# A fp32 decoder layer on one core: more weight sums by DMA at both ends of the feed-forward, token differences made in its first product, tokens prepared two products ahead

## The chip, the core and the metric

One core of a Trainium2 chip runs the whole kernel. The metric is the device time of one execution in microseconds (us), the median over several runs; beside it stands a trace of one profiled execution. The engines are PE (matrix products), DVE (elementwise, also from PSUM banks), ACT (activations and copies), POOL and SP. Here SP issues the loads of weights, and POOL issues the DMAs that add one tile to another.

## What is computed

One layer on 512 tokens of width 1024 in float32: a mixing layer of three head groups, cross-attention into 256 memory tokens, and a feed-forward of width 4096, each as `x = x + RMSNorm(f(RMSNorm(x)))`. The change is in the feed-forward:

```python
h = rms_norm(x, pre_ffn_g[l])
f = jnp.square(jax.nn.relu(h @ w_ff1[l])) @ w_ff2[l]
x = x + rms_norm(f, post_ffn_g[l])
```

## The kernel before

**Arithmetic.** Each float32 operand is split into a high and a low part (`split`, L112: ACT copies the high part, DVE at L115 subtracts it for the low part), and a product is three matmuls: high by low, high by high, low by high. A weight's parts are `fhi` and `flo` of 128x1024; three pairs can live at a time (`HALVES`).

**Seven products for eight.** Both products of the feed-forward work on 2x2 blocks with seven block products p = 1 to 7. They need sums of weight quarters. With quarters r00, r01, r10, r11 the sums are t1 = r00+r01 (used at p = 5), r01 += r11 (p = 7), r00 += r01 (p = 6) and r10 += r00 (p = 4). `Block.sums` makes t1 on DVE (L895), the second sum on DVE (L897) or by a DMA add, and r00 by a DMA add. `Block.of(p)` splits the weights of p and, at p = 6, adds r10 by DMA. All DMA adds (`dma_add`, L868) are issued by POOL, in order; each is 512 KB. The quarters live in 11 slots (`RAWS`): a load waits until the slot's last user is done.

**First product** (`products1`). Eight column groups n of 512 columns, 24 matmuls of 128x256 a product. The order of the work (n, p): p = 1, 2 of groups 0 to 2 (`EARLY`), then group by group (n,5), (n-1,4), (n,6), (n,3), (n,7), from group 3 on with p = 1 and 2 in their places. Weights are prepared two products ahead (`AHEAD`). While it starts, the tokens come from the projection of the cross-attention, one 128-row tile tt at a time: `add_norm`, `norm_a` (DVE L178, then POOL L183 takes a power of one column, then DVE L204 scales two halves), and `put_ff`, which transposes and splits them (DVE L945 and L115). Each finished group is squared into `fq`, which lies in SBUF.

**Second product** (`products2`). Four chunks m of 1024 rows of w_ff2, 24 matmuls of 128x512 a product, p in the order 1, 2, 5, 3, 6, 7, 4 (2, 1, 5, 3, 6, 7, 4 in the last chunk). Its tokens are sums and differences of quarters of `fq` (DVE L1097), split one product ahead, with the weights. Six of the eight PSUM banks keep p = 2, 3, 4 over all chunks; p = 1, 5, 6, 7 share the other two and are drained after each product into `p_sum`: by ACT in chunk 0; for p = 1 and 5 of chunks 1 and 2 by an ACT copy (L1157) and a DMA add; else by a DVE add (L1159). In the last chunk DVE combines the sums into output rows (L1172, L1177), `scaled` multiplies by the gain (L570), and `add_norm` (L178, POOL L183, L577) ends a row tile.

**Order.** A scheduler lays out each engine's program once. It goes by the order of the code and by priorities (`ahead(n)` puts work forward by n), and an engine runs its program in that order: an instruction that waits holds all behind it.

Of the kernel before, what the change touches and what calls it, by code (L numbers as in the profile page):

```python
# [16 lines left out]
P = 128  # L17
# [18 lines left out]
def trunk(ctx: ExitStack, tc: tile.TileContext, a: dict, out: bass.AP):  # L36
# [132 lines left out]
    def gain(src, queue=nc.sync):  # L169
        g = gains.tile([P, D], F32, tag="gain", name=nm("gain"))  # L170
        queue.dma_start(out=g, in_=bass.AP(tensor=src.tensor, offset=src.offset, ap=[[0, P], [1, D]]))
        return g


# [695 lines left out]
    class Block:  # L870


        def __init__(self, shape, src):
            self.shape = shape
            self.src = src
            self.raw = {}

        def load(self, ats, not_before=None):
            for at in ats:
                r = self.raw[at] = self.quarter()  # L880
                with ahead(400):
                    for dst, part in self.src(*at)(r):
                        d = nc.sync.dma_start(out=dst, in_=part)
                        if not_before is not None:
                            tc.add_manual_dep(d.ins, not_before.ins.name, mybir.DependencyInfo(
                                mybir.DependencyClass.NoSync, mybir.DependencyReason.DATA), reason="room")
# [33 lines left out]
    def put_ff(xs, tt):  # L920
# [45 lines left out]
    def group(n):  # L966
# [6 lines left out]
            return parts  # L973
        return Block([P, 4, 256], src)

    def products1(xs):
        work = [(n, p) for n in range(EARLY) for p in (1, 2)]
        for n in range(GROUPS):
            one = [(n, p) for p in ((5, 6, 3, 7) if n < EARLY else (1, 5, 2, 6, 3, 7))]
            work += one[:1] + ([(n - 1, 4)] if n else []) + one[1:]  # L980
        work.append((GROUPS - 1, 4))
        blocks = {}
        ready = {}
# [3 lines left out]
        FIRST, REST = ((0, 0), (1, 0)), ((0, 1), (1, 1))
        for n in range(EARLY):
            blocks[n] = group(n)
            blocks[n].load(FIRST, ff_after[0])  # L990
        blocks[0].load(REST, ff_after[0])

        def prepare(at):

            if at >= len(work):
                return
            n, p = work[at]
            ready[at] = blocks[n].of(p)
            if p == 1 and n >= EARLY:
                blocks[n].sums(False)  # L1000
            if (n, p) == (EARLY - 1, 2):
                blocks[0].sums(False)
            if p == 6 and n + 1 < EARLY:
                blocks[n + 1].sums(False)
            if p == 5 and n + 1 < GROUPS:
                if n + 1 >= EARLY:
                    blocks[n + 1] = group(n + 1)
                    blocks[n + 1].load(FIRST)
                blocks[n + 1].load(REST)

        def out(n, p, ps):

# [31 lines left out]
                else:  # L1044
                    square(quarter(1, 0), two(ps))

        for at in range(AHEAD):
            prepare(at)
        for at, (n, p) in enumerate(work):
            if at in (1, 4):  # L1050
                put_ff(xs[at // 4 + 2], at // 4 + 2)
            prepare(at + AHEAD)
# [16 lines left out]
            out(n, p, ps)  # L1069

    def chunk(m):
        def src(q, i, j):
# [2 lines left out]
                yield t, a["w_ff2"][f:f + 2].rearrange("f p c -> p f c")[:, :, j * 512:(j + 1) * 512]  # L1077
            return parts
        return [Block([P, 2, 512], lambda i, j, q=q: src(q, i, j)) for q in range(2)]

    def products2():
        kept = {p: (bank(), bank()) for p in (2, 3, 4)}
# [26 lines left out]
        def load(m):  # L1109
            if m < NM:  # L1110
                blocks[m] = chunk(m)
                for at in ((0, 0), (1, 0), (0, 1), (1, 1)):
                    for q in range(2):
                        blocks[m][q].load([at])

        def prepare(at):
            if at < len(work):
                m, p = work[at]
                th, tl = tokens(m, p)
                ready[at] = (th, tl, [blocks[m][q].of(p) for q in range(2)])  # L1120
                if p == 1:
                    for q in range(2):
                        blocks[m][q].sums(True)
                if p == 5:
                    load(m + 1)

        load(0)
        def finish(tt, half, y):
            rows[tt][half] = scaled(y, g5[:, HALF[half]])
            if None not in rows[tt]:  # L1130
                add_norm(tt, rows[tt])
                for c in HALF:
# [134 lines left out]
```

## Time and profile before

| | us |
|---|---|
| median of 3 runs | 734.82 (734.81 to 735.44) |
| the profiled execution: its own time | 734.33 |
| its span in the trace | 732.5 |
| PE busy / DVE busy / ACT busy in the span | 695.5 / 530.2 / 433.0 |
| first matmul of the first product | 386.21 |
| first matmul of the last chunk, (3,2) | 675.05 |
| PE's last matmul ends | 717.6 |

The timeline lists instructions by their start. In brackets stands how long the engine was idle before an instruction, and who released it. PEclk is the granted TensorE clock, 1.00 for 2.4 GHz and 0.50 for 1.2 GHz. "Landing" of a DMA is counted from its issue.

### The profile page before, as it was taken

How to read it: one execution, taken by the hardware profiler on the slowest of the kernel's cores; microseconds unless marked ns; L12 is line 12 of the kernel's file. 1: busy time of each engine (PE TensorE's matmuls, PEld its weight loads, DVE VectorE, ACT ScalarE, POOL GpSimd, SP SyncE). 2: the span in 40 equal slices, each digit the busy share in tenths (PEclk: the TensorE clock that was granted, in tenths of full speed). 3: DMA queues.
4: the chain of work that ended last, by engine and by line, in shares of the span. 5: the costliest groups of instructions: out<-in, count | busy, mean ns of one | idle time of the engine just before them, and what ended most of it. 6: DMA issues, size and time to landing. Idle time of an engine off the chain costs nothing.

```text
span 732.5 us, 10699 instructions
## 1 busy us (share of the span) xinstructions
PE 695.5 (95%) x4032; PEld 609.5 (83%) x4032; DVE 530.2 (72%) x803; ACT 433.0 (59%) x776; POOL 132.3 (18%) x143
## 2 busy tenths in 40 slices
PE   8999999997999999999998799999999999999891
PEld 6777888797887889888888799999999888787681
DVE  3479999876774892464469967655666979889797
ACT  5463478797794662353457667666677667375522
POOL 4445343243200110000012010000002021110101
PEclk9999999999999999999999899999999999999997
DMA  8460412143331430011073395567569789695603
GB/s 286 177 230 29 145 40 76 59 158 131 116 114 59 144 115 30 30 57 58 1 223 94 96 221 143 151 168 172 143 179 194 214 186 251 160 247 152 116 0 115
DMA packets 45124, 96.67 MB, mean 132 GB/s; under 512 B 4113, under 2 KB 21265, under 8 KB 45074
## 3 DMA queue, kind: packets, MB, share of 16 engines
q1 hardware_dynamic: 37344, 72.36, 28.9%
q0 software_dynamic: 6336, 23.07, 17.5%
q10 hardware_dynamic: 1394, 0.57, 0.4%
q8 instruction: 31, 0.51, 0.3%
q14 instruction: 19, 0.16, 0.1%
HBM read 70.83 MB, written 2.10 MB: 100 GB/s over the span
## 4 chain that ended last, share of the span: by engine, by line
PE 68%; DVE 17%; ACT 6%; issue 4%; POOL 3%; DMA 2%; DVEq 0%; POOLq 0%; ACTq 0%
PE ps L1067 20%; PE ps L123 15%; PE ps L125 15%; PE ps L124 15%; DVE small L115 2%; DVE flo L115 2%; DVE lo L144 2%; POOL fixed L183 2%; DVE fixed L577 1%; DMA tmp<-in_w_sT 1%; PE ps L685 1%; DVE small L1097 1%; PE ps L697 1%; DVE ps L383 1%; DVE tmp L204 1%
## 5 line engine op out<-in xcount | busy, mean ns | idle before, releaser
L1067 PE MATMUL ps<-small,fhi 128*128 128x256 f32 x896 | 163.8, 285 | 2.7 <-DVE small L115 2.0
L115 DVE TENSOR_TENSOR flo<-quarter,fhi 128x1024 fp32r<-128x1024 f32 x112 | 135.5, 1220 | 38.1 <-ACT fhi L113 34.8
L1067 PEld LDWEIGHTS ps<-small,fhi 128*128 128x128 f32 x896 | 141.2, 194 | 3.8 <-DVE small L115 2.5
L1067 PE MATMUL ps<-small,flo 128*128 128x256 f32 x448 | 127.9, 286 | 3.4 <-DVE flo L115 3.4
L113 ACT ACTIVATE fhi<-quarter 128x1024 fp32r<-128x1024 f32 x112 | 115.3, 1050 | 24.8 <-PE ps L1067 17.2
L123 PE MATMUL ps<-flo,small 128*128 128x512 f32 x224 | 88.2, 394 | 3.3 <-DVE flo L115 2.4
L1067 PEld LDWEIGHTS ps<-small,flo 128*128 128x128 f32 x448 | 86.7, 194 | 4.3 <-DVE flo L115 4.2
L123 PE MATMUL ps<-xl,hi 128*128 128x512 f32 (+1 forms) x256 | 87.3, 341 | 0.5 <-DVE xl L115 0.5
L124 PE MATMUL ps<-fhi,small 128*128 128x512 f32 x224 | 87.7, 392 | 0.0
L125 PE MATMUL ps<-fhi,small 128*128 128x512 f32 x224 | 87.7, 392 | 0.0
L125 PE MATMUL ps<-xh,lo 128*128 128x512 f32 (+1 forms) x256 | 86.3, 337 | 0.4 <-DVE lo L144 0.4
L124 PE MATMUL ps<-xh,hi 128*128 128x512 f32 (+1 forms) x256 | 86.3, 337 | 0.0
L143 ACT ACTIVATE hi<-raw 128x512 fp32r<-128x512 f32 x120 | 70.1, 625 | 14.3 <-PE ps L125 6.8
L868 POOL DMA_DIRECT2D quarter<-quarter x40 | 35.3, 888 | 237.7 <-DVE flo L115 106.5
L144 POOL TENSOR_TENSOR lo<-raw,hi 128x512 fp32r<-128x512 f32 x48 | 63.2, 1331 | 75.7 <-ACT hi L143 66.4
L183 POOL TENSOR_TENSOR fixed<-fixed 128x1 f32<-128x1 f32 x30 | 19.7, 658 | 256.3 <-DVE fixed L178 237.1
L144 DVE TENSOR_TENSOR lo<-raw,hi 128x512 fp32r<-128x512 f32 x72 | 50.6, 732 | 9.7 <-ACT hi L143 9.3
L123 PEld LDWEIGHTS ps<-xl,hi 128*128 128x128 f32 x256 | 48.6, 190 | 5.7 <-issue 0.7
L125 PEld LDWEIGHTS ps<-xh,lo 128*128 128x128 f32 x256 | 48.5, 190 | 5.8 <-DVE lo L144 0.8
L123 PEld LDWEIGHTS ps<-flo,small 128*128 128x128 f32 x224 | 42.3, 189 | 13.2 <-ACT small L113 2.8
L124 PEld LDWEIGHTS ps<-xh,hi 128*128 128x128 f32 x256 | 48.6, 190 | 4.7
L123 PE MATMUL ps<-lo,feat 128*128 128x512 f32 x128 | 50.5, 395 | 0.0
(179 smaller groups left out, 1326.9 us busy)
## 6 DMA issues: line engine op xcount, KB each, us to landing
quarter<-quarter POOLq DMA_DIRECT2D x40, 512.0 KB, 5.2
quarter<-in_w_ff SPq DMA_DIRECT2D x64, 256.0 KB, 4.3
quarter<-in_w_ff SPq DMA_DIRECT2D x32, 512.0 KB, 5.0
raw<-in_w_xk SPq DMA_DIRECT2D x8, 512.0 KB, 3.2
raw<-in_w_xv SPq DMA_DIRECT2D x8, 512.0 KB, 4.2
raw<-in_w_out SPq DMA_DIRECT2D x8, 512.0 KB, 3.5
raw<-in_w_xq SPq DMA_DIRECT2D x8, 512.0 KB, 3.9
raw<-in_w_xo SPq DMA_DIRECT2D x8, 512.0 KB, 4.4
```

Source lines behind the costliest of these rows:

```text
L113: nc.scalar.activation(hi, src, AF.Copy, scale=1.0 if scale is None else scale)
L115: nc.vector.tensor_tensor(out=lo, in0=src, in1=hi.bitcast(F32), op=ALU.subtract)
L123: latest[0] = nc.tensor.matmul(ps, lhsT=lh, rhs=rl, start=start, stop=False)
L124: nc.tensor.matmul(ps, lhsT=lh, rhs=rh, start=False, stop=False)
L125: nc.tensor.matmul(ps, lhsT=ll, rhs=rh, start=False, stop=stop)
L143: nc.scalar.activation(hi, raw[:, c], AF.Copy)
L144: eng.tensor_tensor(out=lo, in0=raw[:, c], in1=hi.bitcast(F32), op=ALU.subtract)
L183: nc.gpsimd.tensor_tensor(out=r, in0=v, in1=neghalf[:, 0:1], op=ALU.pow)
L204: nc.vector.scalar_tensor_tensor(out=xn, in0=src[:, c], scalar=r, in1=g[:, c], op0=ALU.mult, op1=ALU.mult)
L383: nc.vector.scalar_tensor_tensor(out=ac[:, d:], in0=y[:, 0:S - d], scalar=wdw[:, i, CONV - 1 - d:CONV - d], in1=ac[:, d:], op0=ALU.mult, o ...
L868: nc.gpsimd.dma_start(out=out, in_=in_, accum_op=ALU.add)
L1067: nc.tensor.matmul(o, lhsT=w[:, k, c], rhs=x[:, k, :], start=first_, stop=last_, skip_group_check=True)
```

## The change

1. `load_t1`: for groups 0 to 2 of the first product and chunks 2 and 3 of the second, r00 is loaded a second time, and t1 is made from it by a DMA add of r01 instead of by DVE. For groups 0 to 2 the sum r01 += r11 is a DMA add too (`sums(True)`), and group 0's sums are asked for at (0,2), not (2,2).
2. `begin1`: the first weights are loaded and prepared from within `put_ff` of the first token tile.
3. After p = 4 of groups 1 and 3, DVE makes the differences x00-x10 (into `n3`) and x10-x11 (in place) that chunks 0 and 1 of the second product need.
4. Tokens of the second product are split two products ahead (`AHEAD_X`); weights still one.
5. The last gain is loaded in the second product, not ahead of the first.
6. In the last chunk p = 1 and 5 are drained by ACT copies and a DMA add as well.

```diff
+        def load_t1(self, after=None):
+            b00 = self.raw[0, 0]
+            self.load([(0, 0)], after)
+            self.t1, self.raw[0, 0] = self.raw[0, 0], b00
         def sums(self, by_dma):
-            self.t1 = self.quarter()
-            nc.vector.tensor_tensor(out=self.t1, in0=r[0, 0], in1=r[0, 1], op=ALU.add)
+            if self.t1 is None:
+                self.t1 = self.quarter()
+                nc.vector.tensor_tensor(out=self.t1, in0=r[0, 0], in1=r[0, 1], op=ALU.add)
+            else:
+                with ahead(400):
+                    dma_add(self.t1, r[0, 1])
...
         if tt == 0:
             ff_after[0] = latest[0]
+            begin1()
...
+        blocks1[0].load_t1(ff_after[0])
...
-            if (n, p) == (EARLY - 1, 2):
-                blocks[0].sums(False)
+        if (n, p) == (0, 2):
+            blocks1[0].sums(True)
             if p == 6 and n + 1 < EARLY:
-                blocks[n + 1].sums(False)
+            blocks1[n + 1].sums(True)
...
+            blocks1[n + 1].load(REST)
+            if n + 1 < EARLY:
+                blocks1[n + 1].load_t1()
...
+            if p == 4 and n % 2 == 1 and n // 2 < N3S:
...
+                nc.vector.tensor_tensor(out=n3s[m], in0=x00, in1=x10, op=ALU.subtract)
+                nc.vector.tensor_tensor(out=x10, in0=x10, in1=x11, op=ALU.subtract)
...
+            if m in n3s:
+                sums[m, 1], sums[m, 3] = x(1, 0), n3s[m]
...
+                if m >= 2:
+                    for q in range(2):
+                        blocks[m][q].load_t1()
...
+        for at in range(AHEAD_X):
+            prepare_x(at)
         prepare(0)
         for at, (m, p) in enumerate(work):
+            if at == NM:
+                g5.append(gain(a["post_ffn_g"], after=latest[0]))
+            prepare_x(at + AHEAD_X)
             prepare(at + 1)
...
-            part = small([P, 2, 512], F32) if 0 < m < NM - 1 and p in (1, 5) else None
+            part = small([P, 2, 512], F32) if m and p in (1, 5) else None
```

In the changed kernel line numbers are higher: L115 and L945 of the text are L115 and L959 there, L1020 is L1044, L1159 is L1205, L1172 and L1177 are L1218 and L1223, L570 and L577 are L576 and L583, L178 and L183 are L184 and L189, and the DMA adds of L868 stand at L873.

The first place is DVE's program at the start of the first product, from the L178 that belongs to the norm of token tile 2. Before:

```order
L178 TENSOR_SCALAR fixed<-fixed 128x1
L895 TENSOR_TENSOR quarter_4127<-quarter_3957,quarter_3975 128x1024
L204 SCALAR_TENSOR_TENSOR tmp_3894<-fixed,gain_row_3060 128x512
L204 SCALAR_TENSOR_TENSOR tmp_3896<-fixed,gain_row_3060 128x512
L115 TENSOR_TENSOR flo_3982<-quarter_3957,fhi_3981 128x1024
L178 TENSOR_SCALAR fixed<-fixed 128x1
L570 TENSOR_TENSOR tmp_3941<-ps_3898,gain_3058 128x512
L577 SCALAR_TENSOR_TENSOR fixed<-tmp_3705,fixed 128x512
L577 SCALAR_TENSOR_TENSOR fixed<-tmp_3941,fixed 128x512
L115 TENSOR_TENSOR flo_3986<-quarter_3960,fhi_3985 128x1024
```

With the change:

```order
L184 TENSOR_SCALAR fixed<-fixed 128x1
L210 SCALAR_TENSOR_TENSOR tmp_3930<-fixed,gain_row_3060 128x512
L210 SCALAR_TENSOR_TENSOR tmp_3932<-fixed,gain_row_3060 128x512
L184 TENSOR_SCALAR fixed<-fixed 128x1
L576 TENSOR_TENSOR tmp_3977<-ps_3934,gain_3058 128x512
L583 SCALAR_TENSOR_TENSOR fixed<-tmp_3703,fixed 128x512
L583 SCALAR_TENSOR_TENSOR fixed<-tmp_3977,fixed 128x512
L115 TENSOR_TENSOR flo_3866<-quarter_3838,fhi_3865 128x1024
L184 TENSOR_SCALAR fixed<-fixed 128x1
L115 TENSOR_TENSOR flo_3870<-quarter_3841,fhi_3869 128x1024
```

The weight sum of L895 is gone from between the norm's two steps, and the low part of a weight that stood ahead of the projection's gain product now stands behind the two sums into x.

The second place is POOL's program from the 16 powers of the norms on; the quarters' names differ, and the adds are t1, r01, r00 and r10 of a group. Before (three groups' r00 and r10):

```order
L183 TENSOR_TENSOR fixed<-fixed 128x1 x16
L868 DMA quarter_3957<-quarter_3975 128x1024
L868 DMA quarter_3960<-quarter_3957 128x1024
L868 DMA quarter_3963<-quarter_4189 128x1024
L868 DMA quarter_3966<-quarter_3963 128x1024
L868 DMA quarter_3969<-quarter_4324 128x1024
L868 DMA quarter_3972<-quarter_3969 128x1024
```

With the change:

```order
L189 TENSOR_TENSOR fixed<-fixed 128x1 x15
L873 DMA quarter_3862<-quarter_3856 128x1024
L189 TENSOR_TENSOR fixed<-fixed 128x1
L873 DMA quarter_3856<-quarter_3859 128x1024
L873 DMA quarter_3838<-quarter_3856 128x1024
L873 DMA quarter_3841<-quarter_3838 128x1024
L873 DMA quarter_4195<-quarter_4189 128x1024
L873 DMA quarter_4189<-quarter_4192 128x1024
L873 DMA quarter_3844<-quarter_4189 128x1024
L873 DMA quarter_3847<-quarter_3844 128x1024
```

Each of the first three groups now has four DMA adds in a row where it had two, and the first add stands ahead of the last power.

The third place is DVE's program in the last chunk around the last weights (the flo of p = 4, second half). Before, with the drain of p = 7 as the last two rows:

```order
L1159 TENSOR_TENSOR small_5895<-ps_7032,small_5895 128x512
L115 TENSOR_TENSOR flo_7029<-quarter_6607,fhi_7028 128x1024
L1159 TENSOR_TENSOR small_5895<-ps_7033,small_5895 128x512
L115 TENSOR_TENSOR flo_7089<-quarter_6601,fhi_7088 128x1024
L1172 TENSOR_TENSOR small_5895<-small_5893,small_5895 128x1024
L115 TENSOR_TENSOR flo_7093<-quarter_6603,fhi_7092 128x1024
L1159 TENSOR_TENSOR small_5896<-ps_7096,small_5896 128x512
L1159 TENSOR_TENSOR small_5896<-ps_7097,small_5896 128x512
```

With the change, where the drain of p = 7 is L1205:

```order
L1223 TENSOR_TENSOR small_5903<-small_5903,ps_5899 128x512
L1223 TENSOR_TENSOR small_5903<-small_5903,ps_5900 128x512
L576 TENSOR_TENSOR tmp_7081<-small_5903,gain_6121 128x512
L184 TENSOR_SCALAR fixed<-fixed 128x1
L576 TENSOR_TENSOR tmp_7092<-small_5903,gain_6121 128x512
L184 TENSOR_SCALAR fixed<-fixed 128x1
L583 SCALAR_TENSOR_TENSOR fixed<-tmp_6947,fixed 128x512
L583 SCALAR_TENSOR_TENSOR fixed<-tmp_7081,fixed 128x512
L583 SCALAR_TENSOR_TENSOR fixed<-tmp_6952,fixed 128x512
L583 SCALAR_TENSOR_TENSOR fixed<-tmp_7092,fixed 128x512
L1205 TENSOR_TENSOR small_5906<-ps_7109,small_5906 128x512
L115 TENSOR_TENSOR flo_7105<-quarter_6617,fhi_7104 128x1024
```

The last flo now stands behind the drain of p = 7 and behind the end of rows (0,·), L1223 to L583; before, it stood ahead of both.

## Rows read from the trace of the kernel before

**Rows 1.** The page, part 1: busy time, share of the span, instructions.

```profile
PE 695.5 (95%) x4032; PEld 609.5 (83%) x4032; DVE 530.2 (72%) x803; ACT 433.0 (59%) x776; POOL 132.3 (18%) x143
```

**Rows 2.** Busy time by stretch: length, busy (count) per engine, PEclk, DMA share, GB/s.

```profile
405.00:420.00 15.00, 10.51 (x67) 9.89 (x66) 14.97 (x20) 9.82 (x16) 0.87 (x1) 0.77 0.30 80
411.23:418.06 6.83, 4.40 (x21) 4.38 (x21) 6.83 (x8) 2.21 (x3) 0.00 (x0) 0.50 0.23 71
425.00:450.00 25.00, 25.00 (x210) 25.00 (x209) 16.03 (x15) 17.40 (x25) 2.12 (x3) 1.00 0.83 212
560.00:675.00 115.00, 114.15 (x504) 93.93 (x503) 99.63 (x90) 71.12 (x82) 18.49 (x21) 1.00 0.85 206
694.50:697.95 3.45, 3.45 (x10) 2.63 (x9) 3.45 (x4) 1.51 (x2) 0.00 (x0) 0.51 0.00 0
717.00:732.50 15.50, 0.59 (x3) 0.17 (x1) 11.46 (x21) 2.85 (x10) 2.52 (x4) 0.66 0.36 135
```

**Rows 3.** PE's timeline at the start: start, us, line, operation [idle before it, releaser].

```profile
410.15 1.10 PE L1067 MATMUL ps<-small,fhi 128*128 128x256 f32 x4 [1.96 <-DVE small L115]
413.68 0.58 PE L1067 MATMUL ps<-small,flo 128*128 128x256 f32 x1 [2.43 <-DVE flo L115]
```

**Rows 4.** DVE's timeline, same stretch.

```profile
384.62 1.22 DVE L895 TENSOR_TENSOR quarter<-quarter,quarter 128x1024 f32<-128x1024 f32 x1
...
395.26 1.22 DVE L897 TENSOR_TENSOR quarter<-quarter,quarter 128x1024 f32<-128x1024 f32 x1
...
409.41 2.49 DVE L115 TENSOR_TENSOR small<-xf,small 128x512 fp32r<-128x512 f32 x4
```

**Rows 5.** POOL's timeline, same stretch.

```profile
384.85 1.39 POOL L183 TENSOR_TENSOR fixed<-fixed 128x1 f32<-128x1 f32 x1 [2.92 <-DVE fixed L178]
389.09 0.55 POOL L183 TENSOR_TENSOR fixed<-fixed 128x1 f32<-128x1 f32 x1 [2.85 <-DVE fixed L178]
...
397.08 1.06 POOL L868 DMA_DIRECT2D quarter<-quarter  x1 [3.19 <-DVE xf L945]
402.43 0.87 POOL L868 DMA_DIRECT2D quarter<-quarter  x1 [4.29 <-PE ps L1067]
418.70 0.87 POOL L868 DMA_DIRECT2D quarter<-quarter  x1 [15.40 <-DVE quarter L897]
424.45 1.80 POOL L868 DMA_DIRECT2D quarter<-quarter  x2 [4.88 <-DMA quarter<-quarter]
```

**Rows 6.** Line 868, every DMA add of the run: issue to landing.

```profile
DMA to landing us min/median/max: 4.5/5.2/9.8
```

**Rows 7.** The page, part 5, high parts of weights; part 6, their loads (us to landing).

```profile
L113 ACT ACTIVATE fhi<-quarter 128x1024 fp32r<-128x1024 f32 x112 | 115.3, 1050 | 24.8 <-PE ps L1067 17.2
...
quarter<-in_w_ff SPq DMA_DIRECT2D x64, 256.0 KB, 4.3
```

**Rows 8.** DVE's timeline at the fourth column group.

```profile
436.04 1.23 DVE L895 TENSOR_TENSOR quarter<-quarter,quarter 128x1024 f32<-128x1024 f32 x1 [3.43 <-DMA quarter<-in_w_ff]
```

**Rows 9.** PE's waits in the second product: total us, times, longest.

```profile
PE ps L123 <- DVE flo L115: 2.4, 1, 2.4
PE ps L123 <- DVE small L1159: 0.9, 2, 0.4
```

**Rows 10.** PE's timeline in the last chunk: its first matmul, and the late one.

```profile
675.05 0.39 PE L123 MATMUL ps<-flo,small 128*128 128x512 f32 x1
...
693.96 0.47 PE L123 MATMUL ps<-flo,small 128*128 128x512 f32 x1 [2.44 <-DVE flo L115]
```

**Rows 11.** DVE's timeline in the last chunk.

```profile
687.93 1.29 DVE L570 TENSOR_TENSOR tmp<-small,gain 128x512 f32<-128x512 f32 x2
...
710.00 1.22 DVE L115 TENSOR_TENSOR flo<-quarter,fhi 128x1024 fp32r<-128x1024 f32 x1
...
726.58 2.74 DVE L577 SCALAR_TENSOR_TENSOR fixed<-tmp,fixed 128x512 f32<-128x512 f32 x4 [0.50 <-POOL fixed L183]
```

**Rows 12.** DMA issues from 600 to 660 us: adds of partial sums, landing.

```profile
small<-small POOLq DMA_DIRECT2D x4, 512.0 KB, 8.4
```

More of the change, by code (lines that the diff above doesn't have):

```diff
@@ L168, in trunk, with not_before, gain @@
     nc.gpsimd.memset(neghalf, -0.5)
-    def gain(src, queue=nc.sync):
+    def not_before(d, other):
+        if other is not None:
+            tc.add_manual_dep(d.ins, other.ins.name, mybir.DependencyInfo(
+                mybir.DependencyClass.NoSync, mybir.DependencyReason.DATA), reason="room")
+    def gain(src, queue=nc.sync, after=None):
         g = gains.tile([P, D], F32, tag="gain", name=nm("gain"))
-        queue.dma_start(out=g, in_=bass.AP(tensor=src.tensor, offset=src.offset, ap=[[0, P], [1, D]]))
+        not_before(queue.dma_start(out=g, in_=bass.AP(tensor=src.tensor, offset=src.offset, ap=[[0, P], [1, D]])),
+                   after)
         return g
@@ L859, in trunk @@
     HALVES = 3
-    g5 = gain(a["post_ffn_g"])
     fq = [feats.tile([P, 4, S], F32, tag="fq", name=nm("fq"), bufs=8) for _ in range(GROUPS)]
@@ L876, in __init__, with load @@
             self.raw = {}
-        def load(self, ats, not_before=None):
+            self.t1 = None
+        def load(self, ats, after=None):
             for at in ats:
@@ L882, in load @@
                     for dst, part in self.src(*at)(r):
[L883 to L886, printed above, removed]
+                        not_before(nc.sync.dma_start(out=dst, in_=part), after)
+        def load_t1(self, after=None):
+            b00 = self.raw[0, 0]
+            self.load([(0, 0)], after)
+            self.t1, self.raw[0, 0] = self.raw[0, 0], b00
         def quarter(self):
@@ L974, in group @@
         return Block([P, 4, 256], src)
-    def products1(xs):
[L977 to L983, printed above, removed]
+    N3S = 2
+    n3s = {}
+    work1 = [(n, p) for n in range(EARLY) for p in (1, 2)]
+    for n in range(GROUPS):
+        one = [(n, p) for p in ((5, 6, 3, 7) if n < EARLY else (1, 5, 2, 6, 3, 7))]
+        work1 += one[:1] + ([(n - 1, 4)] if n else []) + one[1:]
@@ new lines, in trunk, with begin1, prepare1 @@
+    work1.append((GROUPS - 1, 4))
+    blocks1 = {}
+    ready1 = {}
+    FIRST, REST = ((0, 0), (1, 0)), ((0, 1), (1, 1))
+    def begin1():
+        for n in range(EARLY):
+            blocks1[n] = group(n)
+            blocks1[n].load(FIRST, ff_after[0])
+        blocks1[0].load(REST, ff_after[0])
+        blocks1[0].load_t1(ff_after[0])
+        for at in range(AHEAD):
+            prepare1(at)
+    def prepare1(at):
+        if at >= len(work1):
+            return
+        n, p = work1[at]
+        ready1[at] = blocks1[n].of(p)
+        if p == 1 and n >= EARLY:
+            blocks1[n].sums(False)
+        if (n, p) == (0, 2):
+            blocks1[0].sums(True)
+        if p == 6 and n + 1 < EARLY:
+            blocks1[n + 1].sums(True)
+        if p == 5 and n + 1 < GROUPS:
+            if n + 1 >= EARLY:
+                blocks1[n + 1] = group(n + 1)
+                blocks1[n + 1].load(FIRST)
+            blocks1[n + 1].load(REST)
+            if n + 1 < EARLY:
+                blocks1[n + 1].load_t1()
@@ L984, in products1 @@
+    def products1(xs):
+        work, ready = work1, ready1
         banks = {}
         kept = {}
[L987 to L1000, printed above, removed]
-            if (n, p) == (EARLY - 1, 2):
-                blocks[0].sums(False)
-            if p == 6 and n + 1 < EARLY:
-                blocks[n + 1].sums(False)
[L1005 to L1009, printed above, removed]
@@ L1045, in out @@
                     square(quarter(1, 0), two(ps))
-        for at in range(AHEAD):
-            prepare(at)
         for at, (n, p) in enumerate(work):
@@ L1051, in products1 @@
                 put_ff(xs[at // 4 + 2], at // 4 + 2)
-            prepare(at + AHEAD)
+            prepare1(at + AHEAD)
             wh, wl = ready.pop(at)
@@ L1069, in products1 @@
             out(n, p, ps)
+            if p == 4 and n % 2 == 1 and n // 2 < N3S:
+                m = n // 2
+                x00, x10, x11 = fq[2 * m][:, :, 0:256], fq[2 * m][:, :, 256:512], fq[2 * m + 1][:, :, 256:512]
+                n3s[m] = feats.tile([P, 4, 256], F32, tag="n3", name=nm("n3"), bufs=max(1, N3S))
+                nc.vector.tensor_tensor(out=n3s[m], in0=x00, in1=x10, op=ALU.subtract)
+                nc.vector.tensor_tensor(out=x10, in0=x10, in1=x11, op=ALU.subtract)
     def chunk(m):
@@ L1079, in chunk @@
         return [Block([P, 2, 512], lambda i, j, q=q: src(q, i, j)) for q in range(2)]
+    AHEAD_X = 2
+    g5 = []
     def products2():
@@ L1118, in prepare @@
                 m, p = work[at]
-                th, tl = tokens(m, p)
-                ready[at] = (th, tl, [blocks[m][q].of(p) for q in range(2)])
+                ready[at] = [blocks[m][q].of(p) for q in range(2)]
                 if p == 1:
@@ L1125, in prepare, with prepare_x @@
                     load(m + 1)
+        def prepare_x(at):
+            if at < len(work):
+                ready_x[at] = tokens(*work[at])
         load(0)
         def finish(tt, half, y):
-            rows[tt][half] = scaled(y, g5[:, HALF[half]])
+            rows[tt][half] = scaled(y, g5[0][:, HALF[half]])
             if None not in rows[tt]:
@@ L1133, in finish @@
                     nc.sync.dma_start(out=out[tt * P:(tt + 1) * P, c], in_=x_sb[:, tt, c])
+        ready_x = {}
+        for at in range(AHEAD_X):
+            prepare_x(at)
         prepare(0)
         for at, (m, p) in enumerate(work):
+            if at == NM:
+                g5.append(gain(a["post_ffn_g"], after=latest[0]))
+            prepare_x(at + AHEAD_X)
             prepare(at + 1)
-            th, tl, ws = ready.pop(at)
+            ws = ready.pop(at)
+            th, tl = ready_x.pop(at)
             keeps = p in kept
```

## The prediction

> **What bounds the kernel now.** I read the page first: PE is busy 95% of the span, DVE 72% [rows 1]. So time can only come from stretches in which PE idles or runs at a low clock, and from the end, after PE. The windows by stretch show where these are [rows 2]. From 425 to 450 us PE is full at clock 1.00: 210 matmuls in 25.0 us, 0.119 us each, so a product of 24 takes 2.86 us. In the second product 504 matmuls take 114.15 us, 0.2265 each, 5.44 us a product. Three places stand out.
>
> *Start.* From 405 to 420 us DVE is busy 14.97 of 15 us and PE 10.51, and from 411.23 to 418.06 the clock is 0.50, the 1.2 GHz level [rows 2]. PE's timeline names two waits, 1.96 and 2.43 us, both for DVE [rows 3]; the clock fell behind them. At the low clock 21 matmuls took 4.40 us [rows 2], 0.21 each: 21 x 0.09 = 1.9 us more. Product (0,5) began at 410.15 and ended at about 418.0, where (0,6) began.
>
> *Second product.* PE waits 0.9 us in two pieces for drains, and 2.4 us once for the low part of a weight [rows 9], at 693.96 [rows 10]; the clock is 0.51 for 3.45 us behind that [rows 2], which loses half of it, 1.7 us.
>
> *End.* PE ends at 717.6 (0.59 us after the window's start), and DVE works on [rows 2], to 726.58 + 2.74 = 729.3 [rows 11].
>
> **The change part by part.** I walked each engine's new order with the durations of the rows.
>
> *Start.* Ahead of (0,5) two sums of 1.22 us leave DVE [rows 4], 2.4 us. Beside the first of them a power on POOL took 1.39 us, without one 0.55 [rows 5]: the norm of a token tile gains 0.8. The tokens of p = 5 were ready at 409.41 + 2.49 = 411.9 [rows 4], and the weight that PE lacked stood behind them; now it stands ahead. In the walk some of the 3.2 stays as idle time, (0,5) starts near 410 with no wait inside, the clock stays up, and (0,6) starts at 413.0 and waits 1.0 for ACT and DVE. Gain: 418.0 - 413.0 - 1.0 = 4.0 us.
>
> *What is late next.* Groups 0 to 2 now get t1, r01, r00 and r10 by a chain of four DMA adds each, all on POOL, each waiting for the one before. The price of a link is the question. 424.45 followed 418.70 by 5.75 us and was released by a DMA; 402.43 followed 397.08 by 5.35 and was released by PE, so there a link was at most that [rows 5]. The median landing is 5.2 [rows 6]; the pair at 5.75 shows some 0.4 between landing and the next issue. I take 5.5, between the two pairs, since loads run beside these chains (DMA share 0.83 [rows 2]).
>
> Group 0's chain starts near 389 and has three links done at 406, in time. Group 1's second r00 needs a slot that comes free when (0,5)'s weights are split, 406.3, and lands 4.3 later [rows 7], at 410.6. Its links end at 416.1, 421.6 and 427.1; ACT's copy (1.05 [rows 7]) and the low part (1.22 [rows 4]) make the weights of (1,6) ready at 429.4. PE, six products after (0,5), needs the low part at 428.1: 1.3 us lost. The fourth link lands at 432.6 and frees a slot for the last load of group 3, there at 436.9. That group's two sums, which waited for their load before too (3.43 us [rows 8]), stand on DVE ahead of the low parts for (2,5) and (1,4): 1.8 us lost. Group 2's chain comes behind on POOL: 433.5, 439.0, 444.5, weights of (2,6) at 446.8, needed at 445.3: 1.5 lost. Its fourth link, 450.0, frees the slot for group 4's load (454.3), whose two sums hold the low parts of (2,4) and (3,5): 2.0 lost. Groups 4 and 5 inherit 0.5. Together 7.1 us. Bounds: at a link of 5.0 only 1.6 are lost, by the same walk; at 6.0 it is 11; 0.1 us a link is about 1 us. A gain below nothing is excluded: no add here makes anything ready earlier than DVE did.
>
> *Middle.* In chunks 0 and 1 DVE makes two differences fewer, in chunks 2 and 3 two t1 sums fewer, each 1.22 us as all of this form [rows 4]. The two waits of 0.43 for drains [rows 9] are DVE running late; I count both as gone: -0.9 (at least 0). The two differences per chunk that move into the first product cost nothing, as DVE is busy 16.03 of 25 us there [rows 2]; without that cover 4.9 in all. Four loads and six adds more in the second product meet a DMA share of 0.85 [rows 2]; the sums are used two products, 10.9 us, after their start, which covers an add of 8.4 [rows 12]. Earlier tokens and the later gain load cost PE nothing that I can find.
>
> *Last chunk.* Let T be its first matmul, 675.05 before [rows 10]; products are wanted at T + 5.4, 10.9, 16.3 (p = 3) and 21.8 (p = 6). Four drains leave DVE and tokens come earlier, so the weights of p = 3 are ready at T + 14: the wait at 693.96 and its clock go. But the first output row now waits for p = 1's DMA add, behind eight adds of quarters in POOL's program. ACT's copies end at T + 11.7; alone an add lands in 5.2 [rows 6], those of partial sums took 8.4 [rows 12]: T + 17 to T + 21 with the queue; I take T + 19.4, since no loads for a next chunk run. Behind it on DVE stand two row sums, two gain products (1.29 [rows 11]), the tokens of p = 6, one difference and the low part for p = 6, 5.8 us: (3,6) starts at T + 25.2, 3.4 late, and the clock falls again (1.6).
>
> The last low part was ready at 710.00 + 1.22 [rows 11], before PE's need. Now it stands behind the first drain of p = 7 (its bank is done at T + 36.3), two row sums and gain products, two powers, four row ends (2.74 [rows 11]) and the second drain: at least 8.3 us, T + 44.6. PE wants it at T + 39.0, a quarter into the last product: 5.6 us of wait, then 18 matmuls (4.1) and the low clock: PE ends at T + 50.5, before at T + 42.5. Against that, rows (0,·) are done by then, and DVE ends 4.2 us after PE instead of 11.7: T + 54.7, before T + 54.3. With T + 17 for the add it is 3 us better, with T + 21 1.5 worse; I take +1.0.
>
> **Sum.** -4.0 + 7.1 - 0.9 + 1.0 = +3.2 us on the profiled execution's own 734.33, 737.5; the median of the runs shown lies 0.49 above it, so 738.0.
>
> **Rivals.** About 0.2% (1.5 us) is what a measurement of this kernel tells from no change.
>
> A. *Faster: the adds keep up.* Place: the chains of groups 1 and 2. At 5.0 us a link 1.6 us are lost instead of 7.1, and in the last chunk p = 1's add lands near T + 17, worth some -1: 734.8 - 4.0 + 1.6 - 0.9 - 1.0 = 730.5. The point from which it decides is a link of about 5.15, where the loss is 3. For it: the shortest landing, 4.5 [rows 6], and few loads beside a chain that releases them itself. Against it: the two pairs at 5.35 and 5.75 [rows 5]. Chance 0.20. The Trainium skill's page "DMA: Bandwidth & Descriptors", section "Anatomy of one DMA — SWDGE (gpsimd) path", gives a DMA issued from GpSimd about 2.0 us plus its bytes at 436 per ns, for 512 KB an estimate of 3.2 us; by that this rival would come true, and the chains would cost nothing. The trace does not agree: no add of the run landed under 4.5 us.
>
> B. *Nothing measurable:* links of 5.2 to 5.3, a loss of some 4: 734.8 - 4.0 + 4.3 - 0.9 + 0.3 = 734.5. For it: 5.35 was an upper bound. Chance 0.15.
>
> C. *Much slower: links as beside loads, 5.75 and over.* The loss is 9 or more, and waits of over 1.9 us lower the clock as at the start [rows 3], 1.7 each: 734.8 - 4.0 + 9.5 - 0.9 + 2 + 1.7 = 743. For it: the pair released by a DMA [rows 5]. Chance 0.23.
>
> D. *The change doesn't do what it says:* the first add stands ahead of the last power on POOL, so a late second load of r00 would hold the norm of a token tile, and the start would gain nothing, 742. By the loads' 4.3 [rows 7] it is there before that power is due. Chance 0.02, counted with C.
>
> **How the numbers follow.** The forecast has 0.40, with a range of its own of 736.3 to 740.5, all of it slower. Faster: 0.20. Same: 0.15. Slower: 0.40 + 0.23 + 0.02 = 0.65. Cases of both signs take part, so the range runs from A less 1 to C and a little over, 731.0 to 744.5; a start kept whole and links over 6 us are left out.
>
> **What would show it right or wrong.** Right: no clock below 1.00 from 405 to 420 us; DMA adds of groups 1 and 2 about 5.5 us apart on POOL; PE waits of 1 to 2 us between 428 and 460; none at the two drains in the middle; in the last chunk waits for low parts at p = 6 (3.4) and inside p = 4 (5.6), and DVE ending some 4 us after PE. Wrong: a first product without waits behind 425 us, links under 5.2, a start that still shows half clock, or a last chunk without the wait inside p = 4.

## The result

The changed kernel takes 756.35 us (median of 4 runs, 754.73 to 758.81) against 735.13 for the kernel before (4 runs, 734.81 to 736.76): a ratio of 1.0287, 95% interval 1.0252 to 1.0321. It is 21 us slower. The forecast was slower, 738.0 in a range to 744.5: the sign was right, but of the 21 us it held only 3.

The profiled execution took 755.41 us, its span is 753.7. The page's part 1, and of part 2 the granted clock in 40 slices:

```profile
PE 705.9 (94%) x4032; PEld 618.1 (82%) x4032; DVE 517.4 (69%) x789; ACT 435.6 (58%) x780; POOL 142.9 (19%) x155
...
PEclk9999999999999999999989988999999999999987
```

PE works 10 us longer than in [rows 1] for the same 4032 matmuls, and the granted clock is below 1.00 in more slices: most of this is time at the lower clock. The windows by stretch, columns as in [rows 2]:

```profile
405.00:420.00 15.00, 13.64 (x113) 13.26 (x112) 13.68 (x19) 12.27 (x19) 1.73 (x2) 1.00 0.69 160
415.57:430.00 14.43, 14.41 (x118) 14.21 (x118) 5.62 (x6) 5.19 (x7) 1.72 (x2) 1.00 0.95 247
434.40:440.40 6.00, 6.00 (x28) 6.00 (x29) 3.60 (x3) 3.83 (x6) 0.12 (x1) 0.50 1.05 215
455.10:460.90 5.80, 5.79 (x27) 5.79 (x28) 3.61 (x3) 5.01 (x8) 0.00 (x0) 0.50 0.62 154
676.00:682.00 6.00, 5.09 (x15) 3.77 (x16) 6.00 (x8) 4.17 (x5) 0.20 (x1) 0.72 1.04 241
```

The first line is the start that the change was to mend: 113 matmuls where there were 67, at full clock. In the second PE is still full, but the DMA engines nearly are too. The other three are new losses: twice in the first product some 28 matmuls run at the 1.2 GHz level, and in the second product the clock falls to 0.72 for a stretch.

Four instants split the difference of 21.2 us between the two spans. The first is PE's first matmul of `lo` by `feat`, ahead of everything that the change touches:

```profile
212.04 0.39 PE L123 MATMUL ps<-lo,feat 128*128 128x512 f32 x1
```

```profile
211.06 0.39 PE L123 MATMUL ps<-lo,feat 128*128 128x512 f32 x1
```

| | before | after | later by |
|---|---|---|---|
| first matmul of `lo` by `feat` | 212.04 | 211.06 | -0.98 |
| (0,6) ends | 420.97 | 418.31 | -2.66 |
| second product's first matmul | 556.33 | 568.99 | +12.66 |
| last chunk's first matmul | 675.05 | 692.41 | +17.36 |
| end of the span | 732.5 | 753.7 | +21.2 |

Both kernels run the same instructions up to the first of these, so its 1.0 us is scatter of the execution and no gain. The start gained 1.7, the rest of the first product lost 15.3, chunks 0 to 2 of the second lost 4.7, and the last chunk 3.8.

**First product.** PE's timeline, the waits at (0,5) and at (1,6):

```profile
411.79 0.47 PE L1089 MATMUL ps<-small,fhi 128*128 128x256 f32 x2 [0.91 <-DVE small L115]
...
433.10 0.50 PE L1089 MATMUL ps<-small,fhi 128*128 128x256 f32 x2 [3.11 <-ACT fhi L113]
434.36 0.58 PE L1089 MATMUL ps<-small,flo 128*128 128x256 f32 x1 [0.76 <-DVE flo L115]
```

and at (2,6):

```profile
453.85 0.58 PE L1089 MATMUL ps<-small,fhi 128*128 128x256 f32 x2 [2.40 <-ACT fhi L113]
455.12 0.58 PE L1089 MATMUL ps<-small,flo 128*128 128x256 f32 x1 [0.68 <-DVE flo L115]
```

The first is what is left of [rows 3], with one of 0.45 us at (0,6). The others are new: PE waits for ACT's copy of a weight sum, then for its low part, and behind each pair the clock is at the 1.2 GHz level for some 6 us. POOL's timeline shows what the copies wait for; the first four rows are t1, r01 and r00 of group 1 and, as a pair, r10 of group 1 with t1 of group 2:

```profile
411.63 0.87 POOL L873 DMA_DIRECT2D quarter<-quarter  x1 [7.26 <-DVE xf L959]
416.51 0.86 POOL L873 DMA_DIRECT2D quarter<-quarter  x1 [4.01 <-DMA quarter<-quarter]
423.77 0.86 POOL L873 DMA_DIRECT2D quarter<-quarter  x1 [6.39 <-DMA quarter<-quarter]
432.31 1.78 POOL L873 DMA_DIRECT2D quarter<-quarter  x2 [7.68 <-DMA quarter<-quarter]
440.28 0.86 POOL L873 DMA_DIRECT2D quarter<-quarter  x1 [6.18 <-DMA quarter<-quarter]
447.02 0.86 POOL L873 DMA_DIRECT2D quarter<-quarter  x1 [5.88 <-DMA quarter<-quarter]
453.06 0.88 POOL L873 DMA_DIRECT2D quarter<-quarter  x1 [5.17 <-DMA quarter<-quarter]
```

The distances are 4.88, 7.26 and 8.54 us, then 7.97, 6.74 and 6.04. The pair's second add, t1 of group 2, was issued at 433.03, so its link took 7.25. The DMA view from 415 to 425 us of the changed kernel has the queues (packets, MB, share of the 16 engines; `q0` holds POOL's adds, `q1` SP's loads) and the issues (count, KB each, median us to landing):

```profile
q1 hardware_dynamic: 1615, 1.56, 50.0%
q0 software_dynamic: 192, 0.66, 38.6%
...
quarter<-in_w_ff SPq DMA_DIRECT2D x10, 256.0 KB, 6.9
quarter<-quarter POOLq DMA_DIRECT2D x2, 512.0 KB, 7.5
```

and of the kernel before:

```profile
quarter<-in_w_ff SPq DMA_DIRECT2D x6, 256.0 KB, 3.5
quarter<-quarter POOLq DMA_DIRECT2D x2, 512.0 KB, 5.1
```

Ten loads run beside two links of the chain; before, it was six, and the adds landed in two thirds of the time, the loads in half of it.

**Second product.** PE's waits from chunk 0 to the end, to be set against [rows 9]:

```profile
PE ps L123 <- DVE flo L115: 14.5, 3, 6.4
PE ps L123 <- DVE small L1205: 0.7, 1, 0.7
```

and its three long ones in the timeline, inside p = 6 of chunk 2, ahead of p = 6 of the last chunk, and halfway through the last product:

```profile
676.25 0.79 PE L123 MATMUL ps<-flo,small 128*128 128x512 f32 x1 [3.45 <-DVE flo L115]
...
720.77 0.79 PE L123 MATMUL ps<-flo,small 128*128 128x512 f32 x1 [6.44 <-DVE flo L115]
...
740.64 0.64 PE L123 MATMUL ps<-flo,small 128*128 128x512 f32 x1 [4.58 <-DVE flo L115]
```

The wait of [rows 10] at p = 3 of the last chunk is gone. Of the two waits for drains in [rows 9] one is gone; at p = 7 of chunk 2 0.7 us is left.

### The profile page after: what moved, and what is told of

It reads as the page before. It is cut to its first block, busy times and chain, and to the rows that moved or that the text cites. A ratio compares the mean times of both kernels' runs of the same rounds, so it can differ in the third digit from the quotient of the medians.

```text
span 753.7 us, 10755 instructions
## 1 busy us (share of the span) xinstructions
PE 705.9 (94%) x4032; PEld 618.1 (82%) x4032; DVE 517.4 (69%) x789; ACT 435.6 (58%) x780; POOL 142.9 (19%) x155
## 4 chain that ended last, share of the span: by engine, by line
PE 61%; DVE 12%; DMA 11%; issue 6%; ACT 5%; POOL 2%; SPq 0%; POOLq 0%; DVEq 0%; ACTq 0%
PE ps L1089 14%; PE ps L123 14%; PE ps L125 14%; PE ps L124 14%; DMA quarter<-quarter 6%; DVE flo L115 2%; DVE lo L144 2%; DMA quarter<-in_w_ff 2%; POOL fixed L189 1%; PE ps L691 1%; DVE fixed L583 1%; PE ps L703 1%; DMA tmp<-in_w_sT 1%; DMA fixed<-in_x 1%; DMA small<-small 1%
## 5 line engine op out<-in xcount | busy, mean ns | idle before, releaser
L115 DVE TENSOR_TENSOR flo<-quarter,fhi 128x1024 fp32r<-128x1024 f32 x112 | 135.6, 1221 | 63.8 <-ACT fhi L113 62.2
L1089 PE MATMUL ps<-small,fhi 128*128 128x256 f32 x896 | 169.6, 291 | 8.7 <-ACT fhi L113 6.1
L1089 PEld LDWEIGHTS ps<-small,fhi 128*128 128x128 f32 x896 | 145.8, 200 | 10.2 <-ACT fhi L113 7.0
L1089 PE MATMUL ps<-small,flo 128*128 128x256 f32 x448 | 130.9, 293 | 3.0 <-DVE flo L115 3.0
L123 PE MATMUL ps<-flo,small 128*128 128x512 f32 x224 | 89.7, 401 | 15.3 <-DVE flo L115 14.6
L873 POOL DMA_DIRECT2D quarter<-quarter x50 | 43.8, 882 | 260.4 <-DVE flo L115 87.6
L1089 PEld LDWEIGHTS ps<-small,flo 128*128 128x128 f32 x448 | 89.7, 200 | 3.8 <-DVE flo L115 3.7
L124 PE MATMUL ps<-fhi,small 128*128 128x512 f32 x224 | 88.9, 397 | 0.0
L125 PE MATMUL ps<-fhi,small 128*128 128x512 f32 x224 | 88.7, 396 | 0.0
L189 POOL TENSOR_TENSOR fixed<-fixed 128x1 f32<-128x1 f32 x30 | 19.7, 659 | 244.2 <-DVE fixed L184 224.9
L125 PEld LDWEIGHTS ps<-fhi,small 128*128 128x128 f32 x224 | 43.1, 192 | 9.3
```

The lines of the kernel that those rows point to most:

```text
L115: nc.vector.tensor_tensor(out=lo, in0=src, in1=hi.bitcast(F32), op=ALU.subtract)
L123: latest[0] = nc.tensor.matmul(ps, lhsT=lh, rhs=rl, start=start, stop=False)
L124: nc.tensor.matmul(ps, lhsT=lh, rhs=rh, start=False, stop=False)
L125: nc.tensor.matmul(ps, lhsT=ll, rhs=rh, start=False, stop=stop)
L189: nc.gpsimd.tensor_tensor(out=r, in0=v, in1=neghalf[:, 0:1], op=ALU.pow)
L873: nc.gpsimd.dma_start(out=out, in_=in_, accum_op=ALU.add)
```

## The experiments

Eleven kernels ran; each ratio is to runs of the kernel before on the same chip, whose medians lay at 733.5 to 734.7 us. The first matmul of `lo` by `feat` lies between 209.05 and 213.96 us in the thirteen traces, though no edit stands ahead of it. So one trace is set against another from that instant on.

**1. Early sums back on DVE.**

```diff
-        blocks1[0].load_t1(ff_after[0])
...
-        if (n, p) == (0, 2):
-            blocks1[0].sums(True)
+        if (n, p) == (EARLY - 1, 2):
+            blocks1[0].sums(False)
...
-            blocks1[n + 1].sums(True)
+            blocks1[n + 1].sums(False)
...
-            if n + 1 < EARLY:
-                blocks1[n + 1].load_t1()
```

> The changed kernel, but the t1 and r01 sums of groups 0 to 2 are made by DVE again, as before. Theory (the chains of DMA adds of groups 1 and 2 cost the first product its time): PE reaches the second product 12 to 13 us earlier than in the changed kernel, its waits at (1,6) and (2,6) and the low clock behind them are gone, and the time is 743 to 745. Rival (the other edits of the start, begin1 and the differences on DVE, cost it): at least 752. Rival (both the sums and something else): in between, with waits left in the first product behind 425 us.

743.13 us (ratio to before 1.012, 1.010 to 1.014), 13.2 less than the changed kernel. The second product begins at 556.15, as before the change, and behind 415 us PE waits for nothing in the first product. The theory holds: begin1 and the differences on DVE cost the first product nothing.

**2 to 4. The late t1 undone, the last drains undone, all three undone.**

```diff
# 2 (and 4)
-                if m >= 2:
-                    for q in range(2):
-                        blocks[m][q].load_t1()
# 3 (and 4)
-            part = small([P, 2, 512], F32) if m and p in (1, 5) else None
+            part = small([P, 2, 512], F32) if 0 < m < NM - 1 and p in (1, 5) else None
```

> The changed kernel, but chunks 2 and 3 make t1 on DVE again, with no second load of r00. Theory (the late t1 chains hold POOL's queue and cost the wait of 3.5 us in chunk 2, and delay p = 1's partial sum in chunk 3): 4 to 7 us faster than the changed kernel, 749 to 752, with the wait in chunk 2 gone. Rival (these adds are covered, and the waits come from tokens or drains): within 1.5 us of the changed kernel.

> The changed kernel, but the last chunk drains p = 1 and 5 by DVE adds again. Theory (the first output row waits for p = 1's DMA add, and the weights of p = 6 and 4 wait behind it on DVE): the wait of 6.4 us ahead of p = 6 is gone, 4 to 6 us faster, 750 to 752. Rival (the wait comes from late weight sums): the wait stays, within 1.5 us of the changed kernel.

> The changed kernel without the three parts that use more DMA adds: early sums by DVE, late t1 by DVE, last drains by DVE. What is left is the differences made in the first product, tokens two products ahead, the early begin and the late gain load. Theory (the DMA adds are the whole loss, and the rest saves the drain waits and the wait at p = 3 of the last chunk, 0.9 and up to 4 us): 730 to 734.5. Rival (the rest is worth nothing): 734.5 to 736. Rival (the rest costs too): over 737.

748.21 (1.0201, 1.017 to 1.0232), 748.00 (1.0187, 1.0161 to 1.0214) and 731.00 us (0.9955, 0.9941 to 0.9969). Without the late t1 the wait in chunk 2 is gone and the one ahead of p = 6 falls from 6.4 to 2.7; without the last drains that one is gone, with 0.6 at p = 3, but the one in chunk 2 stays at 2.9. Both waits went as expected, but the times lie 0.8 and 2.0 us below the ranges. Singly the three undone parts give back 13.2, 8.1 and 8.4, together 25.4: the last two share a loss. What is left of the change is faster than the kernel before, by 3.7 between the medians and by 2.4 from `lo` by `feat` to the end of the traces. One long wait stays in number 4, 4.2 us inside the last product; number 3 was expected to show that it belongs to the row that waits for p = 1's add, and it does not.

**5. The last weights first on DVE.** As number 4, with

```diff
-                ready[at] = [blocks[m][q].of(p) for q in range(2)]
+                with ahead(3000 if at == len(work) - 1 else 0):
+                    ready[at] = [blocks[m][q].of(p) for q in range(2)]
```

> The run with all three DMA parts undone, and the weights of the very last product split ahead of the row ends on DVE. Theory (the wait of 4.2 us inside the last product is DVE's order alone, and its cost is partly given back by a shorter end): the wait is gone, PE ends some 5 us earlier, DVE ends 1 to 3 us earlier: 728 to 730.5. Rival (the end is bound by DVE's own work, so the order gives nothing): 731, with DVE ending as long after PE as before the change.

730.37 us (0.9939, 0.9924 to 0.9954). The wait is gone and PE's last matmul starts at 714.23, but DVE's last group now ends 11.3 us after it starts:

```profile
722.81 2.74 DVE L583 SCALAR_TENSOR_TENSOR fixed<-tmp,fixed 128x512 f32<-128x512 f32 x4 [0.32 <-POOL fixed L189]
```

In number 4 it was 5.9 us. What PE waited for was work that must be done anyway: from the last chunk's first matmul PE ends 7.0 us sooner than in number 4, the span only 1.3 (53.2 for 54.5). The gain of 0.6 between the medians is inside the scatter of runs. DVE ends 1 to 3 us earlier, as the theory had it, but nearly as long after PE as before the change, as the rival had it.

**6. Only group 0 by DMA.** As number 5, with the changed kernel's `load_t1` and `sums(True)` for group 0 alone.

> The same as the run before it in this list, and group 0 alone makes t1 and r01 by DMA adds, groups 1 and 2 by DVE. Theory (group 0's chain has time, those of groups 1 and 2 run into a burst of loads): DVE loses 2.4 us ahead of (0,5), the clock stays up there, no waits at (1,6) and (2,6): 3 to 5 us faster than that run, 724 to 727. Rival (any early chain costs, group 0's too, or the four sums of groups 1 and 2 on DVE then hold its queue): not faster than that run.

727.93 us (0.9917, 0.9902 to 0.9932), 2.4 less than number 5 beside it and the fastest of all. The window by stretch at the start of number 5, and of number 6:

```profile
405.00:420.00 15.00, 10.72 (x69) 10.02 (x68) 14.97 (x21) 9.80 (x16) 0.74 (x1) 0.77 0.32 77
```

```profile
405.00:420.00 15.00, 13.63 (x113) 13.26 (x112) 15.00 (x20) 11.55 (x18) 0.87 (x1) 1.00 0.38 100
```

113 matmuls at clock 1.00 in place of 69 at 0.77, and PE is full from 420 to 440: the start is mended, and group 0's chain makes nothing late there. But the two traces differ ahead of the edit:

```profile
212.43 0.39 PE L123 MATMUL ps<-lo,feat 128*128 128x512 f32 x1
```

```profile
210.10 0.39 PE L123 MATMUL ps<-lo,feat 128*128 128x512 f32 x1
```

From there on (0,6) ends 1.7 us sooner than in number 5. Two later waits of 0.6 us for drains cost 1.6, and the second product begins after 344.8 us, in number 5 after 344.9. So 2.3 of the 2.5 us between the two traces lie ahead of the edit, and with six and five runs whose ranges overlap the medians alone do not show a gain either. Shown is that group 0's chain costs nothing; the 3 to 5 us expected did not come.

**7. Tokens one ahead.** As number 4, with `AHEAD_X = 1`.

> All three DMA parts undone, and tokens split only one product ahead, as before. Theory (the wait at p = 3 of the last chunk went by the tokens): that wait of 2.4 us and the low clock are back, and the wait inside the last product is gone; within 1.5 us of the kernel before, 733.5 to 735.5. Rival (the differences made in the first product did it): no wait at p = 3, time as with tokens two ahead, 731.

734.99 us (0.9999, 0.9983 to 1.0014): the gain of number 4 is gone, and the old wait is back, to be set against [rows 10]:

```profile
693.01 0.76 PE L123 MATMUL ps<-flo,small 128*128 128x512 f32 x1 [2.44 <-DVE flo L115]
```

The two waits for drains in the middle, of which number 4 has one of 0.6 us left, are 0.8 and 0.4 us here, though the differences are still made in the first product. So tokens two ahead are what pays, not the differences.

**8. Early t1 by DVE.** The changed kernel without `load_t1` for groups 0 to 2: two links and no second load.

> The changed kernel, but t1 of groups 0 to 2 by DVE; r01 and r00 stay DMA adds. Chains are one link and one load shorter. Theory (serial links that meet a burst of loads): the waits at (1,6) and (2,6) shrink from 3.9 and 3.1 us to under 1 each, the clock stays up, 744 to 748. Rival (the load burst alone, however many links): waits stay over 2 us, over 751.

746.02 us (1.016, 1.0145 to 1.0174). The waits at (1,6) and (2,6) are gone, with 0.9 left inside (2,5), and the second product begins at 556.66. At (0,5) PE waits 4.3 us in three pieces again: the start is not mended. POOL's timeline, r01 and r00 of group 1:

```profile
413.29 0.87 POOL L873 DMA_DIRECT2D quarter<-quarter  x1 [13.80 <-DVE quarter L905]
419.12 0.86 POOL L873 DMA_DIRECT2D quarter<-quarter  x1 [4.96 <-DMA quarter<-quarter]
```

The chain starts later than in the changed kernel, but with one link less its r00 is issued 4.65 us earlier (423.77 there).

**9. The burst held back.** The changed kernel; the loads of groups 2 and 3 wait by a dependency for group 1's r00 add.

```diff
...
-            blocks1[n + 1].load(REST)
+            held[0] = blocks1[1].summed if n + 1 in (2, 3) else None
+            blocks1[n + 1].load(REST, held[0])
...
```

> The changed kernel, but the ten loads of groups 2 and 3 that run beside group 1's chain of adds wait until its r00 add has landed. The chain keeps its three links. Theory (the burst of loads stretches two links to 6.9 and 8.1 us): they land in 4.5 to 5.5 us, the wait at (1,6), 3.1 + 0.8 us, falls under 1 and the clock stays up there; the loads come later, so the wait at (2,6) stays or grows. Rival (three links in series are late whatever runs beside them): links of 5 us, but the wait at (1,6) stays over 2 us.

POOL's timeline, group 1's four adds:

```profile
412.69 0.87 POOL L874 DMA_DIRECT2D quarter<-quarter  x1 [6.40 <-DVE small L115]
417.56 0.86 POOL L874 DMA_DIRECT2D quarter<-quarter  x1 [4.00 <-DMA quarter<-quarter]
422.42 0.86 POOL L874 DMA_DIRECT2D quarter<-quarter  x1 [4.00 <-DMA quarter<-quarter]
427.32 0.88 POOL L874 DMA_DIRECT2D quarter<-quarter  x1 [4.04 <-DMA quarter<-quarter]
```

Three links of 4.87, 4.86 and 4.90 us, where it was 4.88, 7.26 and 8.54; no load is issued between 409 and 427 us. ACT's copy of the weights of (1,6), here and in the changed kernel:

```profile
427.00 1.06 ACT L113 ACTIVATE fhi<-quarter 128x1024 fp32r<-128x1024 f32 x1 [2.83 <-DMA quarter<-quarter]
```

```profile
431.99 1.06 ACT L113 ACTIVATE fhi<-quarter 128x1024 fp32r<-128x1024 f32 x1 [8.51 <-DMA quarter<-quarter]
```

PE does not wait at (1,6) at all. The theory holds: three links in series are in time when nothing runs beside them. The held loads come too late instead: group 2's t1 add waits for one until 437.89, ACT's next copy waits for the add, and a drain that PE needs stands behind that copy. PE waits 10.7 us once, and at (2,6) 2.0 and 0.8 stay:

```profile
447.15 0.80 PE L1092 MATMUL ps<-small,fhi 128*128 128x256 f32 x2 [10.72 <-ACT tmp L1056]
```

762.46 us in all (1.0394, 1.0367 to 1.0422).

**10 and 11. One part alone, beside number 4.** Number 4 with the change's last drains, and number 4 with its late t1.

> Early and late sums by DVE as before the change, the last chunk's drains of p = 1 and 5 by ACT and DMA as in the change. Theory (the first output row waits for p = 1's add, which is late by itself): wait of 2 to 3 us ahead of p = 6 of the last chunk, 3 to 5 us slower than the run with all three undone, 734 to 736. Rival (the add is late only behind the late t1 adds): 731, no wait over 1 us there.

> Early sums and last drains by DVE as before the change, t1 of chunks 2 and 3 by DMA as in the change. Theory (each late t1 chain delays the r00 of its chunk): a wait of about 3 us in chunk 2, none over 1 us ahead of p = 6 of the last chunk, 3 to 5 us slower than the run with all three undone, 734 to 736. Rival (covered by itself): 731.

734.15 (1.0005, 0.999 to 1.002) and 735.19 us (1.0020, 1.0005 to 1.0035): 3.2 and 4.2 over number 4, with waits of 2.5 us ahead of p = 6 and 2.6 us in chunk 2. Waits and medians are as expected. Together they cost 12.1 (number 1 less number 4), so 4.8 us come only from both. That figure is rough: the kernel before took 1.2 us less beside these two than beside number 4, which leaves 2.4, and from `lo` by `feat` the traces give 0.9 and 3.9 of 10.8, which leaves 6.0. ACT's last copy of p = 1, POOL's add and DVE's first row sum, in number 10:

```profile
686.39 0.60 ACT L1197 ACTIVATE small<-ps 128x512 f32<-128x512 f32 x1 [0.76 <-PE ps L125]
```

```profile
687.39 1.01 POOL L873 DMA_DIRECT2D small<-small  x1
```

```profile
693.80 1.29 DVE L1217 TENSOR_TENSOR small<-small,ps 128x512 f32<-128x512 f32 x2 [3.47 <-DMA small<-small]
```

and the same in the changed kernel:

```profile
703.49 0.60 ACT L1203 ACTIVATE small<-ps 128x512 f32<-128x512 f32 x1 [0.76 <-PE ps L125]
```

```profile
707.37 0.87 POOL L873 DMA_DIRECT2D quarter<-quarter  x1 [1.65 <-DMA quarter<-quarter]
707.91 1.22 POOL L873 DMA_DIRECT2D small<-small  x1
```

```profile
714.83 1.28 DVE L1223 TENSOR_TENSOR small<-small,ps 128x512 f32<-128x512 f32 x2 [7.40 <-DMA small<-small]
```

Alone, the add is issued 0.4 us after the copies end (686.99), and DVE goes on 6.8 us after them. With the late t1 it is issued 3.8 us after them, as the quarters' adds ahead of it come one by one, and DVE goes on 10.7 after.

## Why the prediction was wrong, point by point

Term by term, forecast and measured: the start -4.0 and -1.7, the chains +7.1 and +15.3, the middle -0.9 and +4.7, the last chunk +1.0 and +3.8.

*The chains: right in mechanism, wrong in size.* The step that failed is the price of a link, "I take 5.5, between the two pairs, since loads run beside these chains". One price does not do: a link alone is 4.9 us (number 9), one beside the burst 7.3 to 8.5. Group 1's chain began at 411.63, 1.0 later than forecast, and its three links took 20.3 us to the last landing and not 16.5. With r00 landed at 431.9 and not at 427.1, the wait at (1,6) was 3.9 us and not 1.3, at (2,6) 3.1 and not 1.5. The waits forecast at (2,5) and (2,4) did not come; that PE was late enough for them by then is argued, not tried. The burst meets the chain because both wait for group 0: from 405 to 430 us SP waits 23.1 us, 22.2 of it for DVE's low parts, whose quarters' slots the loads need.

The kernel before had shown a dear link. [rows 5] merges two adds at 424.45, and the second of them, group 2's r00, ran beside another add and six loads. Its landing in the view of line 868:

```profile
DMA to landing us min/median/max: 8.1/8.1/8.1
```

The 0.4 us between landing and issue is no reading of the pair, whose 5.75 less 5.2 is 0.55; number 9 shows 0.35 to 0.41, so little hangs on it.

*The clock behind the waits.* The forecast's 7.1 us held none of it; only rival C had it. Behind (1,6) the clock stayed low from 434.4 to 440.4, behind (2,6) from 455.1 to 460.9: some 28 matmuls each at 0.21 us in place of 0.119, 2.5 us each. With the waits and the slow first matmuls between them, (1,6) cost 7.1 us, (2,6) 6.2 and a wait of 1.2 us for a drain at 507.88 1.5: 14.8 of the 15.3. Rival C named both links and clock, and at 9.5 + 1.7 was still short.

*The start.* 1.7 instead of 4.0. The clock stayed up, as forecast, and the low part stood ahead. But the 2.4 and 0.8 us that left DVE and the norm brought the tokens no sooner. The four token splits that began at 409.41 in [rows 4]:

```profile
410.96 2.49 DVE L115 TENSOR_TENSOR small<-xf,small 128x512 fp32r<-128x512 f32 x4
```

So (0,5) began at 411.79, not 410. What was gained is the wait inside (0,5) and the low clock behind it; that PE waited 0.45 and not 1.0 at (0,6) helped.

*The middle.* "The sums are used two products, 10.9 us, after their start, which covers an add of 8.4" failed. It covers one add, and the late t1 makes a chain of three: the adds of one half of chunk 2 are issued at 649.3, 656.18 and 663.73, and the last lands 10.1 us later, 24.5 after the first was issued. Number 11 shows 2.6 us of wait in chunk 2 and some 4 us of time from this alone. Of the two waits for drains only one went, and by the tokens, not by the differences on DVE (number 7).

*The last chunk.* T + 19.4 for p = 1's add, then the wait ahead of p = 6, then the last low part behind the row ends: all came in this order. The add was issued late, behind the quarters' adds (numbers 10 and 11). It let DVE go on at T + 22.4, past the bound of T + 21, and the wait was 6.4 us instead of 3.4. The 5.2 us for an add alone was a misreading: [rows 6] gives the median of all adds, and alone one lands in 4.5 (number 9). The wait inside the last product was 4.6 instead of 5.6: the low part was there at T + 48.2 and not at T + 44.6, but PE had done half of the product by then, 12 of 24 matmuls, and not a quarter. DVE's last rows:

```profile
736.11 2.74 DVE L583 SCALAR_TENSOR_TENSOR fixed<-tmp,fixed 128x512 f32<-128x512 f32 x4 [0.34 <-POOL fixed L189]
...
739.37 1.22 DVE L115 TENSOR_TENSOR flo<-quarter,fhi 128x1024 fp32r<-128x1024 f32 x1
...
749.32 1.41 DVE L583 SCALAR_TENSOR_TENSOR fixed<-tmp,fixed 128x512 f32<-128x512 f32 x2 [0.44 <-POOL fixed L189]
```

The flo at 739.37 stands behind the four row ends of 736.11 and the drain of p = 7 (738.77), as the order had it. DVE ends 5.5 us after PE's last matmul has ended, near the 4.2 forecast. +3.8 in place of +1.0.

*The rivals.* A's links of 5.0 exist, but only without neighbours. By the Trainium skill's page "DMA: Bandwidth & Descriptors", section "Anatomy of one DMA — SWDGE (gpsimd) path", a DMA of 512 KB takes an estimated 3.2 us; the shortest add of number 9 landed in 4.5, so the trace does not agree even without load. D, a second load of r00 that holds the norm, did not occur: the first add was issued at 387.85, and the last power at 390.75 waited for DVE. The range's lower end does not follow from its words: "A less 1" is 729.5, not 731.0; nothing hangs on it, as the result lies above the upper end.

## What to carry to other kernels

An add that moves from an engine to a DMA queue is cheap only where one of them is needed and time lies before its use: a chain of such adds pays each link in full, and pays most where freed slots release a burst of loads. Price such a link by what will run beside it at that moment, alone and in the burst, and not by a mean of the trace. Then add the low clock behind each wait of PE that comes out: here 2.5 us behind waits of 3.9 and 3.1. A change of several parts is worth taking apart: here tokens two ahead gave some 4 us (number 4 against number 7), and the three uses of DMA adds took 25. And set two traces against each other from an instant ahead of the edit: here up to 4.9 us lay before it, more than the tokens were worth.

## What was not expected of the hardware

Adds of 512 KB with nothing beside them follow each other on POOL in 4.86 to 4.90 us, 4.5 of it landing. Beside ten loads of 256 KB the same adds took 7.26 and 8.54, and the loads 6.9 instead of 3.5. The DMA engines were nearly full then, with a share of 0.95 at 247 GB/s, where the stretch from 375 to 390 us of the same run, mostly loads, moved 319 at 1.01. The queues show why the same share moves less: from 415 to 425 us the adds took 38.6% of the engines' time for 0.66 MB and the loads 50.0% for 1.56. Alone, in number 9 from 412.6 to 427 us, it is:

```profile
q0 software_dynamic: 432, 1.57, 57.8%
```

An estimate from these two rows and the load's: a byte that is added takes the engines 1.7 to 1.8 times as long as a byte that is loaded. Which part of an add takes that time was not tried.
